# Rotary sines and cosines computed in the mixer's first phase, from a small load of their own

## The chip, the cores and the metric

One Trainium2 chip; the kernel uses one of its cores. The metric is device time in microseconds (us), the median of several runs. The engines are named as in the profile: PE is TensorE (PEld its weight loads), DVE is VectorE, ACT is ScalarE, POOL is GpSimd, and SP is SyncE, whose queue issues nearly all loads.

## The reference

A decoder block on 256 tokens of width 1024. All that the change touches is the rotary embedding of the retention branch:

```python
def rotary(x, positions):
    half = x.shape[-1] // 2
    inv = ROPE_BASE ** (-jnp.arange(half, dtype=jnp.float32) / half)
    ang = positions.astype(jnp.float32)[..., None] * inv
    cos = jnp.cos(ang)[:, :, None, :]
    sin = jnp.sin(ang)[:, :, None, :]
...
def mixer(...):
    proj = xm @ w_in        # 16 blocks of 512 columns, and 8 gate columns
    ml_qk = jax.nn.silu(causal_dwconv(ml_qk, conv_w, conv_b))
    h_ml = mlstm_chunkwise(...)          # needs the gates and the convolved q, k
    ret_q = rotary(ret_q ...); ret_k = rotary(ret_k ...)
    h_ret = retention_chunkwise(...)
...
x = x + gate_m * mixer(rmsnorm(x) * (1 + scale_m) + shift_m)
x = x + gate_f * moe(...)                # top 4 of 32 experts
```

The table of angles is 256 positions by 64 frequencies; in the kernel it is two tiles of 128 tokens side by side, 128x128.

## The kernel before

**Products.** Every weight tile of the mixer is split in two: ACT copies it to a rounded high half (`split_high`, L369, `partsa`), DVE subtracts to get the low half (`split_low`, L374, `partsb`), and PE multiplies high by high, low by high and high by low. Each half has a ring of four 128x512 slots, so ACT may run at most four splits ahead of PE. PE takes its products in the order in which they are written.

**First phase.** The modulation of the input comes in four steps `s`, each a quarter of the channels (two groups `k` of 128). A step multiplies the two groups that are ready by their rows of `qk0`, `qk1` (both L415 to L417) and `v0`, and in between makes the next two groups ready (`ada_mm`, `modulated`). Inside this phase PE, DVE and ACT run in the order in which the code is written (`tc.manual_schedule(engines=engines)`); an engine takes its instructions strictly in that order.

**Second phase.** Four more projections follow, `v1`, `rqk0`, `rqk1`, `rv0`, eight splits each (`projections`). Beside them runs `side`, a chain of generators: `gates` (the log-sigmoid of the forget gate: Exp, Ln, a reciprocal and two scans on DVE and ACT), `conv(1)`, `tables`, `gates_to_columns`, `weights_of_scores`, `scores`; PE takes one step of it after each projection product. In this phase only PE's order is written out; a scheduler sets the order on DVE and ACT, and SP's as well, and it may draw in work that is written later, such as `expert_biases` (three rounded levels `b` of the expert biases `braw`, L853, their differences L855, and 16 small copies issued on ACT, L857).

**The table.** `tables` casts the positions (`post`, an own load at L450) to `posf` (L525), multiplies them by the frequencies `inv`, reduces the angle to one turn, and takes two sines; sines and cosines land in the tile U1b. `inv` is 64 columns of the constants `cb`, which are loaded after the first phase, into memory that the first phase uses for other things. The angles live in a ring of three slots in U6b (`t2`). `rotated` reads the finished table.

**Loads.** SP issues loads one after another, each under one of eight completion semaphores in turn: the ninth load waits until the first has landed.

**After the mixer** come the router and 16 pairs of experts, whose weights (2 MB loads `gu`, `dn`) go into the mixer's weight slots as these come free.

Of the kernel before, what the change touches and what calls it, by code (L numbers as in the profile page):

```python
# [112 lines left out]
def block(ctx, tc, I, out, dbg=None):  # L113
    nc = tc.nc
    pe, dve, act, pool, sp = nc.tensor, nc.vector, nc.scalar, nc.gpsimd, nc.sync
# [111 lines left out]
    with ExitStack() as mctx:  # L227
# [43 lines left out]
        cb = U2b[:, 768:1988]  # L271
# [82 lines left out]
        qi = U1b[:, 512:1024].rearrange("p (h j) -> p h j", h=H)  # L354
        SR = U1b[:, 1024:1280]
        gc = U1b[:, 1280:1536].rearrange("p (c q) -> p c q", c=2)
        cs_ = U1b[:, 1536:1664].rearrange("p (t i) -> p t i", t=2)
        sn_ = U1b[:, 1664:1920].rearrange("p (t s i) -> p t s i", t=2, s=2)
        U3a = region("U3a", [128, 2048], "U3a")
        U3b = region("U3b", [128, 2048], "U3b")  # L360
        U4a = region("U4a", [128, 2056], "U4a")
# [90 lines left out]
        decay = cb[:, 128:640]  # L452
        kdec = cb[:, 640:644]
        qdec = cb[:, 644:1156]
        inv = cb[:, 1156:1220]

        wifs = sb(m, [128, 2, 416], "wifs", F32R, tag="gm")
        pool.memset(f32v(wifs), 0.0)
# [10 lines left out]
        def chain_of(*gens):  # L469
            for g in gens:  # L470
                yield from g
# [7 lines left out]
        def slow(gen):  # L479
            for _ in gen:  # L480
                yield
                yield
# [206 lines left out]
        with tc.manual_schedule(engines=engines):  # L689
# [53 lines left out]
            for s in range(4):  # L743
                ks = (2 * s, 2 * s + 1)
                p1 = [split(wq1[:, k:k + 1], f"qk1q{k}") for k in ks]
                for k, part in zip(ks, p0):
                    productsT(oqk[0], k, part)
                if s < 3:
                    scol = ada_mm(*SCALE[s + 1])
                else:  # L750
                    act.activation(warm, csil[:, 0:1], AF.Silu)
                    gate_weights()
                    side = conv(0)
                p2 = [split(wv0[:, k:k + 1], f"v0q{k}") for k in (ks[:1] if s < 3 else ks)]
                for k, part in zip(ks, p1):
                    productsT(oqk[1], k, part)
                if s == 3:
                    advance(side, 9)
                else:
                    p2.append(split(wv0[:, ks[1]:ks[1] + 1], f"v0q{ks[1]}"))  # L760
                    scol()
                    scale(s + 1)
                    shift = ada_mm(*SHIFT[s + 1])
                products1(ov0, ks[0], p2[0], hh)
                if s < 3:
                    p0 = [split(wq0[:, k:k + 1], f"qk0q{k}") for k in (2 * s + 2, 2 * s + 3)]
                    shift()
                    for k in (2 * s + 2, 2 * s + 3):
                        modulated(k)
                products1(ov0, ks[1], p2[1], hh)  # L770
        with tc.manual_schedule(engines={pe.engine}):
            held["wv1"] = wslot(win(3), "v1")
            sp.dma_start(cb, I["const_b"])
            for z in range(2):
                held[f"wrqk{z}"] = wslot(win(6 + z), f"rqk{z}")
            held["wrv0"] = wslot(win(8), "rv0")
            gate_products()
            main = projections()
            values(0, ov0)
            side = chain_of(gates(), slow(conv(1)), tables(), gates_to_columns(), weights_of_scores(), scores())  # L780
            for i in main:
                if i == 15:
                    side = both(side, rotated(0))
                if i == 23:
                    side = both(side, rotated(1))
                if i > 0:
                    advance(side)
            advance(side, 99)
            dbg("qT", qT)
            dbg("kT", kT)  # L790
            dbg("SR", SR)
            dbg("EX", EX4)
            dbg("Cs", Cs)
            dbg("nS", nS)
# [701 lines left out]
```

## Time and profile before

| | |
|---|---|
| median of 3 runs | 1243.28 us (1243.12 to 1244.7) |
| profiled execution | 1242.2 us, span 1240.4 us |
| busy, share of the span | PE 94%, DVE 39%, ACT 24%, POOL 1% |
| mean granted TensorE clock | 0.996 of full |
| bytes moved | 479.12 MB, 386 GB/s |

The span is what the profiler saw from the first to the last instruction; the profiled execution's own time is 1.8 us longer than it. The mixer takes the first 300 us, the experts the rest. A mean over the whole span says little about the change, which lies between 40 and 95 us; the stages there have to be read one by one.

### The profile page before, as it was taken

The numbers are of one execution on the slowest core, as the hardware profiler recorded it, in microseconds if no ns is written. First come the engines' busy times: TensorE is split into PE (matmuls) and PEld (weight loads), VectorE is DVE, ScalarE is ACT, GpSimd is POOL, SyncE is SP. The second block draws the span as 40 slices with busy tenths as digits, with TensorE's granted clock in tenths as the row PEclk, the third lists the DMA queues.
The fourth block names the chain that finished last, engine by engine and source line by source line (L and its number), as shares of the span: only waits on it lengthen the run. The fifth ranks groups of instructions, "written<-read, shape, count | busy, mean of one in ns | idle before, by whom it ended". The sixth has DMA issues, their size and how long they took to land.

```text
span 1240.4 us, 14605 instructions
## 1 busy us (share of the span) xinstructions
PE 1168.6 (94%) x5886; PEld 583.2 (47%) x5887; DVE 487.1 (39%) x1149; ACT 292.5 (24%) x575; POOL 7.8 (1%) x18
## 2 busy tenths in 40 slices
PE   8999999999999999999998989898989898989996
PEld 7878888888634334343332324232423233332333
DVE  5599889968422222222222222122212121312123
ACT  4585655565211101111110101010101010110112
POOL 0000000000000000000000000000000000000001
PEclk9999999999999999999999999999999999999999
DMA  9956789948999999999999999999999999999995
GB/s 365 368 181 210 273 301 350 365 174 334 350 430 428 428 427 428 427 428 429 425 427 429 427 428 426 427 430 427 426 428 429 427 426 429 427 427 428 426 421 214
DMA packets 44030, 479.12 MB, mean 386 GB/s; under 512 B 5554, under 2 KB 6514, under 8 KB 12980
## 3 DMA queue, kind: packets, MB, share of 16 engines
q1 hardware_dynamic: 42948, 477.01, 92.9%
q10 hardware_dynamic: 1008, 1.12, 0.3%
q8 instruction: 48, 0.79, 0.3%
q14 instruction: 26, 0.21, 0.1%
HBM read 476.46 MB, written 1.05 MB: 385 GB/s over the span
## 4 chain that ended last, share of the span: by engine, by line
DMA 54%; PE 43%; DVE 1%; ACT 1%; SPq 0%; issue 0%; ACTq 0%
PE gup L1260 10%; PE dnp L1297 5%; DMA gu123b<-in_w 3%; DMA gu83b<-in_w 3%; DMA gu63b<-in_w 3%; DMA gu103b<-in_w 3%; DMA gu151b<-in_w 3%; DMA gu91b<-in_w 3%; DMA gu131b<-in_w 3%; DMA gu143b<-in_w 3%; DMA dn131b<-in_w 3%; DMA dn71b<-in_w 3%; DMA gu111b<-in_w 3%; DMA dn51b<-in_w 3%; DMA dn91b<-in_w 3%; DMA gu71b<-in_w 3%
## 5 line engine op out<-in xcount | busy, mean ns | idle before, releaser
L1169 DVE TENSOR_SCALAR g<-gup 128x256 f32<-128x256 f32 x64 | 27.2, 425 | 344.0 <-PE gup L1260 344.0
L1249 ACT ACTIVATE aT<-aTp 128x256 f32<-128x256 f32 x64 | 24.5, 383 | 285.5 <-PE aTp L1248 285.5
L1170 ACT ACTIVATE sg<-g 128x256 f32<-128x256 f32 x64 | 26.7, 416 | 255.4 <-DVE g L1169 255.4
L1133 PEld LDWEIGHTS xgp<-oh,x 128*128 128x128 f32 x512 | 61.9, 191 | 49.6 <-issue 25.2
L1139 DVE TENSOR_SCALAR xg<-xgp,fsc,fsh 128x128 f32<-128x128 f32 x64 | 26.2, 409 | 146.7 <-ACT xg L1141 146.7
L1133 PE MATMUL xgp<-oh,x 128*128 128x128 f32 x512 | 73.7, 287 | 0.0
L1304 DVE SCALAR_TENSOR_TENSOR yp<-dnp,wsl,gf 128x512 f32<-128x512 f32 (+2 forms) x34 | 24.5, 719 | 111.9 <-PE dnp L1297 110.1
L1141 ACT ACTIVATE xg<-xgp,fsh,fsc 128x128 f32<-128x128 f32 x64 | 29.0, 453 | 150.6 <-PE xgp L1133 150.6
L1316 ACT ACTIVATE yph<-yp 128x512 fp32r<-128x512 f32 x31 | 19.5, 630 | 93.9 <-DVE yp L1304 93.9
L1248 PEld LDWEIGHTS aTp<-ca,a 128*128 128x128 f32 x128 | 13.7, 142 | 39.2 <-issue 39.2
L1173 DVE TENSOR_TENSOR a<-a,sg 128x256 f32<-128x256 f32 x64 | 27.2, 425 | 7.5 <-ACT sg L1170 1.0
L1172 DVE SCALAR_TENSOR_TENSOR a<-a,g 128x256 f32<-128x256 f32 x64 | 27.2, 425 | 2.1
L1322 PE MATMUL ya<-yph,ohT 128*128 128x512 f32 x62 | 27.8, 448 | 0.0
L1248 PE MATMUL aTp<-ca,a 128*128 128x128 f32 x128 | 27.4, 296 | 0.0
L1171 DVE TENSOR_SCALAR a<-gup 128x256 f32<-128x256 f32 x64 | 26.5, 415 | 0.0
L1159 DVE TENSOR_SCALAR ohT<-cwp 128x256 fp32r<-128x256 f32 x16 | 6.8, 424 | 49.1 <-PE cwp L1158 49.1
L1317 DVE TENSOR_TENSOR ypl<-yp,yph 128x512 fp32r<-128x512 f32 x31 | 21.3, 689 | 11.9 <-ACT yph L1316 11.9
L224 PE MATMUL gup<-bex,id 96*64 96x512 bf16 x128 | 25.1, 387 | 0.0
L1322 PE MATMUL ya<-ypl,ohT 128*128 128x512 f32 x62 | 24.6, 396 | 0.0
L1322 PEld LDWEIGHTS ya<-yph,ohT 128*128 128x128 f32 x62 | 11.6, 187 | 26.1 <-issue 24.3
L224 PEld LDWEIGHTS <-id 96*64 96x64 bf16 x196 | 11.6, 109 | 25.1 <-issue 22.3
L1125 DVE TENSOR_SCALAR oh<-ca,posm,rc 128x64 f32<-128x64 f32 x64 | 17.0, 309 | 4.6 <-PE xgp L1133 4.6
(902 smaller groups left out, 2317.6 us busy)
## 6 DMA issues: line engine op xcount, KB each, us to landing
gu00a<-in_w SPq DMA_DIRECT2D x1, 2048.0 KB, 7.7
gu00b<-in_w SPq DMA_DIRECT2D x1, 2048.0 KB, 7.5
gu01a<-in_w SPq DMA_DIRECT2D x1, 2048.0 KB
gu01b<-in_w SPq DMA_DIRECT2D x1, 2048.0 KB, 7.6
gu02a<-in_w SPq DMA_DIRECT2D x1, 2048.0 KB
gu02b<-in_w SPq DMA_DIRECT2D x1, 2048.0 KB, 12.6
gu03a<-in_w SPq DMA_DIRECT2D x1, 2048.0 KB
gu03b<-in_w SPq DMA_DIRECT2D x1, 2048.0 KB
```

Source lines behind the costliest of these rows:

```text
L224: pe.matmul(p[rows, :c1 - c0], id3[:, e:e + 1].to_broadcast([96, CAP]), bex[:, n, c0:c1], start=True, stop=False, skip_group_check=True)
L1133: pe.matmul(p[:, q * 128:(q + 1) * 128], x[:, t, k * 128:(k + 1) * 128], oh[:, t].rearrange("p q s -> p (q s)"), start=t == 0, stop=t == 1)
L1141: act.activation(xg[:, k], pq, AF.Identity, bias=fsh[:, k:k + 1], scale=fsc[:, k:k + 1])
L1169: dve.tensor_scalar(g[:r], v[:, 0], LIMIT, None, op0=OP.min)
L1170: act.activation(sg[:r], g[:r], AF.Sigmoid, scale=ALPHA)
L1171: dve.tensor_scalar(a[:r], v[:, 1], LIMIT, -LIMIT, op0=OP.min, op1=OP.max)
L1172: dve.scalar_tensor_tensor(a[:r], a[:r], 1.0, g[:r], op0=OP.add, op1=OP.mult)
L1173: dve.tensor_mul(a[:r], a[:r], sg[:r])
L1248: pe.transpose(p[:, q * 128:(q + 1) * 128], a[:, q * 128:(q + 1) * 128], ident)
L1260: pe.matmul(p[q * CAP:(q + 1) * CAP], xg[:, k, q * CAP:(q + 1) * CAP], w[q, k, slice(0, 512)], start=False, stop=k == 7, skip_group_check= ...
L1297: pe.matmul(p[q * CAP:(q + 1) * CAP, :c1 - c0], aT[:, k, q * CAP:(q + 1) * CAP], w[q, k, slice(c0, c1)], start=False, stop=k == 7, skip_gr ...
L1322: pe.matmul(yacc[t][n], ohT[:, t * 128:(t + 1) * 128], part, start=pair == i == 0, stop=i == 1 and pair >= NP - 2, skip_group_check=True)
```

## The change

The table gets a tile of its own, `rot`, instead of a part of U1b, and the frequencies get a tile and a load of their own, issued right behind the load of the positions. All of `tables()` is run at the end of step `s == 1` of the first phase, behind `modulated` of that step and ahead of the splits of `qk1` of the next one. The chain `side` has one generator less.

```diff
--- before.py
+++ after.py
@@ -354,8 +354,9 @@
         qi = U1b[:, 512:1024].rearrange("p (h j) -> p h j", h=H)
         SR = U1b[:, 1024:1280]
         gc = U1b[:, 1280:1536].rearrange("p (c q) -> p c q", c=2)
-        cs_ = U1b[:, 1536:1664].rearrange("p (t i) -> p t i", t=2)
-        sn_ = U1b[:, 1664:1920].rearrange("p (t s i) -> p t s i", t=2, s=2)
+        rot = sb(m, [128, 384], "rot")
+        cs_ = rot[:, 0:128].rearrange("p (t i) -> p t i", t=2)
+        sn_ = rot[:, 128:384].rearrange("p (t s i) -> p t s i", t=2, s=2)
         U3a = region("U3a", [128, 2048], "U3a")
         U3b = region("U3b", [128, 2048], "U3b")
         U4a = region("U4a", [128, 2056], "U4a")
@@ -452,7 +453,8 @@
         decay = cb[:, 128:640]
         kdec = cb[:, 640:644]
         qdec = cb[:, 644:1156]
-        inv = cb[:, 1156:1220]
+        inv = sb(m, [128, 64], "inv")
+        sp.dma_start(inv, I["const_b"][:, 1156:1220])
 
         wifs = sb(m, [128, 2, 416], "wifs", F32R, tag="gm")
         pool.memset(f32v(wifs), 0.0)
@@ -768,6 +770,9 @@
                     for k in (2 * s + 2, 2 * s + 3):
                         modulated(k)
                 products1(ov0, ks[1], p2[1], hh)
+                if s == 1:
+                    for _ in tables():
+                        pass
         with tc.manual_schedule(engines={pe.engine}):
             held["wv1"] = wslot(win(3), "v1")
             sp.dma_start(cb, I["const_b"])
@@ -777,7 +782,7 @@
             gate_products()
             main = projections()
             values(0, ov0)
-            side = chain_of(gates(), slow(conv(1)), tables(), gates_to_columns(), weights_of_scores(), scores())
+            side = chain_of(gates(), slow(conv(1)), gates_to_columns(), weights_of_scores(), scores())
             for i in main:
                 if i == 15:
                     side = both(side, rotated(0))
```

On DVE in the first phase the code's order decides. These are its rows before, at the end of step s=1: `hb` is the low half of the modulated input, `partsb<-wfirst1b` the low halves for `qk1` of step s=2.

```order
L440 TENSOR_TENSOR hb<-U2b,ha 128x256
L374 TENSOR_TENSOR partsb<-wfirst1b,partsa 128x512 x2
L313 COPY U6b<-ada_544 128x128
L374 TENSOR_TENSOR partsb<-wfirst2b,partsa 128x512 x2
L303 TENSOR_TENSOR mod<-adac_583,cols 128x2
```

And with the change, at the same place (`post` are the positions, `rot` the table):

```order
L441 TENSOR_TENSOR hb<-U2b,ha 128x256
L527 CAST posf<-post 128x2
L530 TENSOR_SCALAR U6b<-inv,posf 128x64 x2
L535 TENSOR_SCALAR U6b<-U6b 128x128
L536 TENSOR_SCALAR U6b<-U6b 128x128
L538 SCALAR_TENSOR_TENSOR U6b<-U6b 128x128 x3
L540 TENSOR_SCALAR U6b<-U6b 128x128
L545 TENSOR_TENSOR U6b<-U6b 128x128
L546 TENSOR_SCALAR rot<-U6b 128x128
L547 TENSOR_SCALAR rot<-rot 128x2x64
L375 TENSOR_TENSOR partsb<-wfirst1b,partsa 128x512 x2
```

The twelve instructions of the table now stand between `hb` and the two low halves; the row `CAST` needs the positions' load, and the row behind it that of `inv`.

On DVE in the second phase the scheduler decides. Before, from the reciprocal of the gates on (`nS` and `U1a` hold gates, `partsb` are low halves for `v1` and `rqk0`, `U2b` the convolution):

```order
L562 RECIPROCAL nS<-nS 4x256
L374 TENSOR_TENSOR partsb<-v1b,partsa 128x512
L563 TENSOR_TENSOR nS<-nS 4x256
L374 TENSOR_TENSOR partsb<-rqk0a,partsa 128x512
L565 TENSOR_TENSOR nS<-nS 4x256
L374 TENSOR_TENSOR partsb<-rqk0a,partsa 128x512
L566 SCALAR_TENSOR_TENSOR nS<-nS 4x256
L504 SCALAR_TENSOR_TENSOR U2b<-qk1p_294,cols,U2b 128x254
L572 SCALAR_TENSOR_TENSOR U1a<-nS 4x128 x2
L504 SCALAR_TENSOR_TENSOR U2b<-qk1p_294,cols,U2b 128x255
L573 SCALAR_TENSOR_TENSOR U1a<-fi,bif,U1a 4x256
L374 TENSOR_TENSOR partsb<-rqk0a,partsa 128x512
```

With the change:

```order
L564 RECIPROCAL nS<-nS 4x256
L375 TENSOR_TENSOR partsb<-v1b,partsa 128x512
L565 TENSOR_TENSOR nS<-nS 4x256
L375 TENSOR_TENSOR partsb<-v1b,partsa 128x512
L567 TENSOR_TENSOR nS<-nS 4x256
L506 SCALAR_TENSOR_TENSOR U2b<-qk1p_297,cols,U2b 128x253
L568 SCALAR_TENSOR_TENSOR nS<-nS 4x256
L506 SCALAR_TENSOR_TENSOR U2b<-qk1p_297,cols,U2b 128x254
L574 SCALAR_TENSOR_TENSOR U1a<-nS 4x128 x2
L506 SCALAR_TENSOR_TENSOR U2b<-qk1p_297,cols,U2b 128x255
L575 SCALAR_TENSOR_TENSOR U1a<-fi,bif,U1a 4x256
L375 TENSOR_TENSOR partsb<-rqk0a,partsa 128x512
```

One more low half of `v1` now stands behind the reciprocal, and the first of `rqk0` has moved from the second place behind it to the last row shown, behind most of the gates' chain. Further on, ahead of the first low half of `rqk0b`, stand three differences of `braw` that before stood behind all of `rqk1`.

On ACT in the second phase, before, from the first high half of `v1b` to the logarithm (L557 is the gates' Exp, L560 their Ln, L499 the Silu of the convolution):

```order
L369 ACTIVATE partsa<-v1b 128x512
L499 ACTIVATE U3a<-U2b 128x256
L497 ACTIVATE U2b<-qk1p_295,cols 128x256
L369 ACTIVATE partsa<-v1b 128x512
L557 ACT_TABLE_LOAD
L557 ACTIVATE nS<-nS 4x256
L369 ACTIVATE partsa<-v1b 128x512 x2
L560 ACT_TABLE_LOAD
L560 ACTIVATE nS<-nS 4x256
L499 ACT_TABLE_LOAD
L499 ACTIVATE U3a<-U2b 128x256
```

With the change (line numbers up by two; L858 and L862 are `expert_biases`):

```order
L858 ACTIVATE b_2322<-braw_1247 128x512
L499 ACTIVATE U2b<-qk1p_297,cols 128x256
L862 DMA bex<-b_2322 32x512 x3
L501 ACTIVATE U3a<-U2b 128x256
L862 DMA bex<-b_2322 32x512
L370 ACTIVATE partsa<-v1b 128x512
L559 ACT_TABLE_LOAD
L559 ACTIVATE nS<-nS 4x256
L501 ACT_TABLE_LOAD
L501 ACTIVATE U3a<-U2b 128x256
L370 ACTIVATE partsa<-v1b 128x512
L562 ACT_TABLE_LOAD
```

A bias level and four copies have come in ahead of the first high half of `v1b`, and one Silu now stands between Exp and Ln, with a table load of its own.

## Rows read from the trace of the kernel before

**Rows 1.** The page: its span, and the shares of the chain that ended last

```profile
span 1240.4 us, 14605 instructions
...
DMA 54%; PE 43%; DVE 1%; ACT 1%; SPq 0%; issue 0%; ACTq 0%
```

**Rows 2.** Stages of the mixer: length, busy time per engine (instructions), PEclk, DMA share

```profile
70.00:85.00 15.00, 12.29 (x52) 9.03 (x51) 13.79 (x30) 12.65 (x22) 0.00 (x0) 1.00 0.43 139
85.00:300.00 215.00, 214.27 (x1017) 177.39 (x1016) 192.47 (x386) 124.97 (x215) 0.00 (x0) 1.00 0.75 279
```

**Rows 3.** TensorE in order of time, first products of `qk1` in step s=2

```profile
45.21 0.28 PE L416 MATMUL qk1p<-ha,partsb 128*128 128x256 f32 x1
45.33 0.28 PE L417 MATMUL qk1p<-hb,partsa 128*128 128x256 f32 x1
```

**Rows 4.** VectorE in order of time: first low half for those products; the cast

```profile
41.88 0.69 DVE L374 TENSOR_TENSOR partsb<-wfirst1b,partsa 128x512 fp32r<-128x512 f32 x1
...
57.74 0.16 DVE L525 CAST posf<-post 128x2 f32<-128x2 int32 x1
```

**Rows 5.** SyncE's queue in order of time, around the positions' load

```profile
40.86 0.40 SPq L450 DMA_DIRECT2D post<-in_positions  x1
42.20 0.36 SPq L170 DMA_DIRECT2D v1a<-in_win  x1
```

**Rows 6.** DMA issues from 30 to 46 us: KB, us from issue to landing

```profile
v1a<-in_win SPq DMA_DIRECT2D x1, 1024.0 KB, 5.3
...
post<-in_positions SPq DMA_DIRECT2D x1, 1.0 KB, 4.3
```

**Rows 7.** VectorE on the tile U6b, 66 to 94 us: ns min/median/max

```profile
L536 DVE SCALAR_TENSOR_TENSOR U6b<-U6b x3: 269/273/273, 89.8 to 91.1; 128x128 f32<-128x128 f32 x3
...
L528 DVE TENSOR_SCALAR U6b<-U2b,posf x2: 232/240/247, 69.3 to 87.8; 128x64 f32<-128x64 f32 x2
...
L533 DVE TENSOR_SCALAR U6b<-U6b x1: 208/208/208, 88.6 to 88.6; 128x128 f32<-128x128 f32 x1
```

**Rows 8.** ScalarE on the tile U6b, 66 to 94 us

```profile
L540 ACT ACTIVATE U1b<-U6b x1: 293/293/293, 92.7 to 92.7; 128x128 f32<-128x128 f32 x1
```

**Rows 9.** ScalarE in order of time, its first two entries

```profile
0.78 1.28 ACT L690 ACT_TABLE_LOAD   x1 [0.64 <-PEq L1484]
3.08 0.21 ACT L690 ACTIVATE csil<-ca 128x8 f32<-128x8 f32 x1 [1.02 <-DMA ca<-in_const_a]
```

**Rows 10.** TensorE in order of time, two of its waits in the second phase

```profile
80.80 0.50 PE L387 MATMUL rqk_p<-partsb,ha 128*128 128x512 f32 x1 [1.18 <-DVE partsb L374]
...
84.58 0.50 PE L387 MATMUL rqk_p<-partsb,ha 128*128 128x512 f32 x1 [0.63 <-DVE partsb L374]
```

**Rows 11.** ACT and DVE in order of time, from the gates' Exp to their reciprocal

```profile
69.81 1.15 ACT L369 ACTIVATE partsa<-v1b 128x512 fp32r<-128x512 f32 x2
...
70.98 1.28 ACT L560 ACT_TABLE_LOAD   x1
...
72.28 0.42 ACT L560 ACTIVATE nS<-nS 4x256 f32<-4x256 f32 x1
...
70.29 0.48 DVE L504 SCALAR_TENSOR_TENSOR U2b<-qk1p,cols,U2b 128x253 f32<-128x253 f32 x1
...
72.72 1.74 DVE L562 RECIPROCAL nS<-nS 4x256 f32<-4x256 f32 x1 [0.78 <-ACT nS L560]
```

**Rows 12.** The tile b (bias levels), 55 to 130 us: ns min/median/max

```profile
L857 ACTq DMA_DIRECT2D bex<-b x16: 514/515/605, 90.3 to 129.0; - x16
L853 ACT ACTIVATE b<-braw x5: 615/622/632, 89.6 to 127.6; 128x512 bf16<-128x512 f32 x3, 64x512 bf16<-64x512 f32 x2
L855 DVE TENSOR_TENSOR braw<-braw,b x3: 630/680/687, 104.4 to 126.0; 128x512 f32<-128x512 f32 x2, 64x512 f32<-64x512 f32 x1
```

**Rows 13.** The end of the run, columns as in rows 2

```profile
1230.00:1232.00 2.00, 0.40 (x4) 0.21 (x2) 1.02 (x6) 0.55 (x3) 0.00 (x0) 1.00 0.03 8
...
1236.00:1238.00 2.00, 0.00 (x0) 0.00 (x0) 0.00 (x0) 0.00 (x0) 0.00 (x0) 0.50 0.78 309
```

## The prediction

> **What bounds the kernel now.** I read the page first. The chain of work that ended last is DMA for 54% and PE for 43% [rows 1]: the expert stage streams its weights to the end, and before it PE sets the pace. The expert loads start when mixer slots come free, so a microsecond won or lost in the mixer moves the whole stream, one for one. The table by stage shows where the mixer can move. From 85 to 300 us PE is busy 214.27 of 215.00; from 70 to 85 us it idles 2.71 of 15.00, while DVE is busy 13.79 [rows 2]. PE's own rows say what for: low halves that DVE had not finished, 1.18 us at 80.80 and 0.63 us at 84.58 [rows 10]. The table's costly part stands at 88 to 94 us in the run before [rows 7], where PE has no idle time that could be given back.
>
> **Term 1: the table in the first phase.** Added are one load, and on DVE twelve instructions; on ACT two sines and a table load. They stand ahead of the low halves for `qk1` of step s=2. The first of these starts at 41.88 now [rows 4], and PE uses it at 45.21 [rows 3]: 2.6 us of slack beyond its 0.69.
>
> DVE's first new row casts the positions. Their load is issued at 40.86 [rows 5] and takes 4.3 us [rows 6], behind large loads in the same queue, so it lands at 45.2. Nothing ahead of it on SP changes, so DVE, which goes on in order, stands still from about 42.0 to 45.2 although it has nothing else to wait for. The frequencies follow on SP at the place that the load of `v1a` holds now, 42.20 [rows 5], when the next of the eight semaphores is free. No row shows this load. Lower bound: it lands with the positions, 45.2. Upper bound: 5.3 us like `v1a`, 1 MB issued at the same moment [rows 6], that is 47.5. It is 32 KB, so I take it near the lower end, 45.4. The loads behind it move back by one place; that is hidden, since `v1a` has landed at 47.5 and its first low half comes after the cast at 57.74 [rows 4, 6].
>
> From 45.4 the DVE chain is dependent, so durations add, each from its twin of the run before [rows 7]: two products with the frequencies, the second overlapped (0.25 + 0.15), two of 0.21, three of 0.27, a clamp of 0.21: 1.84, and some 0.2 for eight handovers. 47.45. Then ACT: the sine whose result is squared starts about 0.2 behind the first and takes 0.29 [rows 8]: 48.0. The table load costs nothing if it runs ahead of its operand. The very first one did: it ran at 0.78, and the instruction behind it then sat idle for 1.02 until its load [rows 9]. The lower bound is 0, the upper 1.28 [rows 11]; I take 0, as ACT is idle there while it waits for DVE. DVE then squares (about 0.27) and makes cosines and the negated sines (0.21 each, overlapped), to 48.7 [rows 7]; ACT has the high half by 48.5, DVE the low half at 48.7 + 0.7 = 49.4. PE's second matmul of `qk1` starts at 49.4 instead of 45.21: **4.2 us late**. The bounds are 4.0 and 6.3 from the two landings, 7.6 if the table load waits too.
>
> PE cannot make this up. The splits, convolutions and gates behind it depend on what PE does in this phase, and the four slots keep ACT and DVE from running far ahead.
>
> **Term 2: the second phase.** Taken from it are the cast (0.16), the twelve-row chain of some 2.6, and two sines. All but the cast and one product (0.25) stood at 88 us or later, where PE is full: worth nothing. Ahead of the first low half of `rqk0b`, for which PE waits at 84.58, the new order puts three bias differences, 0.63 to 0.69 each [rows 12], 2.0 in all, that stood at 104 us and later. Less the 0.41 removed that is +1.6 us on DVE, in its busiest stretch.
>
> Second, the gates. The reciprocal overwrites what Ln reads, so it waits for ACT: 0.78 us now [rows 11]. Between the end of Exp and the end of Ln ACT did two splits, one table load and Ln, 1.15 + 1.28 + 0.42 = 2.85. With the change it does a table load, a Silu, a split, another table load and Ln: 1.28 + 0.42 + 0.57 + 1.28 + 0.42 = 3.97 [rows 11], so 1.1 more. DVE filled that time before with two taps of the convolution, 0.48 each [rows 11], that now come ahead of Exp. Its idle time grows by 1.1 + 0.96, about 2.0. Together **3.6 us** by which the low half of `rqk0b`, and PE with it, comes later. From there PE is full and the lead that DVE regains is not used.
>
> ScalarE: Activation LUTs of the Trainium skill (section What ACT_TABLE_LOAD costs) would make each switch of tables dearer, about 2.66 us, of which 1.38 is a drain behind the load. The rows show no drain: the load at 70.98 takes 1.28 and its activation starts at 72.28 [rows 11]. By the page the one extra load would add 1.4 us to the sum; I go by the row.
>
> The bounds of term 2 are -2.7 (all of PE's idle time from 70 to 85 us is recovered [rows 2], because the relief came earlier than the order shows) and +5 (the four copies and the bias levels on ACT, 0.51 and 0.62 each [rows 12], delay high halves too). The two sums above go row by row through the new order, so I take 3.6.
>
> **Sum.** 4.2 + 3.6 = 7.8 on the profiled execution's 1242.2 (span 1240.4 and 1.8 around it) is 1250.0. The median of the runs shown, 1243.28, is 1.1 higher, so I name 1251.0.
>
> **Rivals.**
> *Only the first term.* The second phase hides its new waits under others: 1243.3 + 4.2 = 1247.5. For it: DVE and ACT both have small gaps from 70 to 85 us [rows 2]. Against: the gaps of DVE are waits for ACT, and both get more work.
>
> *The clock falls in the stall.* TensorE stands nearly still for some 4 us. The rows show one fall: PE had its last work in 1230 to 1232 at clock 1.00, and the clock is 0.50 in 1236 to 1238 [rows 13], which is 1.2 of 2.4 GHz. If the stall does the same, the 24 `qk1` products behind it, 0.12 apart [rows 3], take 2.9 us more: 1254. Against: PE was idle longer there. TensorE: Matmul & The Clock Gate of the Trainium skill (section The HAM clock gate) says that an idle array falls to half rate and gets the full rate back after sustained work; the end of the run agrees, and no row shows whether this stall is enough.
>
> *Not slower: the relief reaches PE.* Place: the low halves from 70 to 85 us. If DVE without the table delivers them in time, PE's 2.71 us of idle time go, and with the stall of 4.2 the time is 1244.8, within 0.2%. It decides from a gain of 1.7 us on. To end faster, the positions and frequencies would also have to have landed by 42: then the table costs 0.9 beyond the slack of term 1 (0.2 + 2.0 on DVE, 0.6 for the sines, 0.7 for the last three, against 2.6), and the time is 1241.5, still inside the bound. Against: the removed rows stood behind that stretch.
>
> **Chances.** Forecast, both terms (including a late `inv` or the dearer table load, up to 1254): 0.55. Only the first: 0.22. Clock: 0.13. Relief: 0.10, of which 0.02 stands for a gain of over 0.2%, which needs 0.7 us more than the best case just named. The range 1247.0 to 1254.5 leaves out the relief and what of the clock and a late landing adds up. What a measurement of this kernel can tell from no change is about 0.2%, 2.5 us. So slower 0.90, same 0.08, faster 0.02.
>
> **What would show it.** Right: DVE idle before the cast until about 45.2, released by the load of the positions or of `inv`; the table load on ACT near 41.2, with no wait; PE's `qk1` low product of s=2 at about 49.4; the first `rqk0b` low product near 92.4 instead of 84.58; PE full from there on, and the last 900 us the same but shifted. Wrong: the cast at 42; a granted clock below 1.00 from 49 us on; the first `rqk0b` product within 4.5 us of 84.58, which would cancel term 2; or new waits for loads in the mixer, whose order on SP has changed.

## The result and the profile after

The median after is 1254.2 us (six runs, 1253.33 to 1255.34), against 1243.47 us before (six runs beside them, 1243.12 to 1244.7). The ratio is 1.0084, with a 95% interval of 1.0074 to 1.0094: slower by 10.7 us. The profiled execution of after took 1254.67 us, so its span is 12.3 us longer than that of before [rows 1]; two single executions differ by their own scatter too. One execution of e7 below took 5756 us, at full clock and for no known cause, and its median and ratio go by the other five. The page after, its span and the shares of the chain that ended last:

```profile
span 1252.7 us, 14602 instructions
...
DMA 57%; PE 39%; DVE 2%; ACT 2%; issue 0%; SPq 0%; ACTq 0%; DVEq 0%
```

The loss lies in the mixer. Stages of after, columns as in [rows 2]:

```profile
45.00:50.00 5.00, 1.00 (x10) 0.36 (x2) 3.52 (x14) 1.55 (x4) 0.00 (x0) 0.73 0.92 320
50.00:55.00 5.00, 5.00 (x27) 5.00 (x27) 1.97 (x4) 1.31 (x3) 0.00 (x0) 0.59 0.99 397
55.00:60.00 5.00, 5.00 (x36) 3.51 (x37) 3.02 (x9) 2.59 (x6) 0.31 (x1) 1.00 0.79 264
70.00:85.00 15.00, 11.97 (x55) 8.99 (x54) 10.21 (x18) 11.87 (x20) 0.96 (x1) 1.00 0.55 204
```

Two things are new. PE does 1.00 us of work in 45 to 50, and its granted clock is 0.73 there and 0.59 in the next five. From 70 to 85 DVE is busy for 10.21 us instead of 13.79 [rows 2]: it has less to do and waits, so another engine is late.

**The first phase.** VectorE of after in order of time, from the cast to the first low half of `qk1` for s=2:

```profile
45.58 0.17 DVE L527 CAST posf<-post 128x2 f32<-128x2 int32 x1 [3.32 <-DMA post<-in_positions]
...
48.59 0.29 DVE L545 TENSOR_TENSOR U6b<-U6b 128x128 f32<-128x128 f32 x1 [0.57 <-ACT U6b L543]
...
49.19 1.28 DVE L375 TENSOR_TENSOR partsb<-wfirst1b,partsa 128x512 fp32r<-128x512 f32 x2
```

DVE stood still for 3.32 us. What it waited for, in SyncE's queue and in the view of DMA issues (KB, us to landing):

```profile
41.40 0.40 SPq L451 DMA_DIRECT2D post<-in_positions  x1
42.67 0.36 SPq L457 DMA_DIRECT2D inv<-in_const_b  x1
```

```profile
inv<-in_const_b SPq DMA_DIRECT2D x1, 32.0 KB, 3.1
...
post<-in_positions SPq DMA_DIRECT2D x1, 1.0 KB, 4.2
```

41.40 + 4.2 = 45.6 and 42.67 + 3.1 = 45.8: the two loads land nearly together, and the chain of the table runs from there to 49.2. ScalarE's table load for the sines cost nothing, as it ran ahead of its operand:

```profile
41.46 1.28 ACT L542 ACT_TABLE_LOAD   x1
48.05 0.31 ACT L542 ACTIVATE rot<-U6b 128x128 f32<-128x128 f32 x1 [5.30 <-DVE U6b L540]
```

TensorE behind it, the products of `qk1` for s=2 that answer to [rows 3], the last of them, and what follows:

```profile
49.12 0.58 PE L416 MATMUL qk1p<-ha,partsa 128*128 128x256 f32 x1 [3.77 <-ACT partsa L370]
49.93 0.58 PE L417 MATMUL qk1p<-ha,partsb 128*128 128x256 f32 x1 [0.22 <-DVE partsb L375]
50.30 0.41 PE L418 MATMUL qk1p<-hb,partsa 128*128 128x256 f32 x1
50.52 0.41 PE L416 MATMUL qk1p<-ha,partsa 128*128 128x256 f32 x1
...
54.13 0.28 PE L418 MATMUL qk1p<-hb,partsa 128*128 128x256 f32 x1
54.25 0.28 PE L416 MATMUL qk1p<-ha,partsa 128*128 128x256 f32 x1
...
54.61 0.50 PE L301 MATMUL adac<-ca,U6b 128*128 128x1 f32 x4
```

The second product starts at 49.93 instead of 45.21. The starts then lie 0.21 apart until 53.9, and 0.12 apart after that: the clock's lower level, 1.2 of 2.4 GHz. Of the 24 products, 18 went by at that pace. From 49.93 to the `adac` behind these products it is 4.68 us; before, it was 2.75 (45.21 to 47.96), so the clock cost 1.9.

**The second phase.** ScalarE of after, from the first bias level to the gates' Ln (the counterpart of [rows 11]):

```profile
70.49 0.63 ACT L858 ACTIVATE b<-braw 128x512 bf16<-128x512 f32 x1 [0.41 <-DMA braw<-in_bgu]
...
71.15 2.77 ACTq L862 DMA_DIRECT2D bex<-b  x3
73.97 0.42 ACT L501 ACTIVATE U3a<-U2b 128x256 f32<-128x256 f32 x1 [2.39 <-DVE U2b L506]
...
75.25 1.28 ACT L559 ACT_TABLE_LOAD   x1
76.55 0.42 ACT L559 ACTIVATE nS<-nS 4x256 f32<-4x256 f32 x1
...
79.23 1.28 ACT L562 ACT_TABLE_LOAD   x1
80.53 0.42 ACT L562 ACTIVATE nS<-nS 4x256 f32<-4x256 f32 x1
```

The first level waits 0.41 us for its own load. Three DMA issues then fill ScalarE's queue until 73.92 (71.15 + 2.77), and the Silu behind them starts at 73.97. Its idle time of 2.39 us is put down to a tap of DVE (a step of the convolution), since the profile counts no issue as work. That tap had ended by about 72.3, so some 1.7 us of the wait are the issues'; the row above it shows what the engine did. All issues, in the groups of the tile `b` [rows 12], as ns min/median/max:

```profile
L862 ACTq DMA_DIRECT2D bex<-b x18: 514/515/1496, 71.2 to 117.6; - x18
```

One takes 515 ns as a rule, and the third of these 1496. There were 18 in the kernel before too (two of them behind the window of [rows 12]), so only their place is new. With them ScalarE was full from 70 to 85: 11.87 us of busy time, 2.77 of issues, and 0.57 for a fourth at 73.98 make 15.2 of 15.00, the little too much being overlap. Before, all issues stood behind 90 us [rows 12].

TensorE's waits of this phase, the last two of which answer to [rows 10]:

```profile
79.27 0.49 PE L387 MATMUL v_p<-partsa,ha 128*128 128x512 f32 x1 [1.23 <-ACT partsa L370]
...
83.49 0.50 PE L388 MATMUL v_p<-partsb,ha 128*128 128x512 f32 x1 [1.34 <-DVE partsb L375]
...
88.84 0.50 PE L388 MATMUL rqk_p<-partsb,ha 128*128 128x512 f32 x1 [2.33 <-DVE partsb L375]
...
92.62 0.50 PE L388 MATMUL rqk_p<-partsb,ha 128*128 128x512 f32 x1 [0.63 <-DVE partsb L375]
96.41 0.50 PE L388 MATMUL rqk_p<-partsb,ha 128*128 128x512 f32 x1 [0.23 <-DVE partsb L375]
```

The last two are smaller than their twins before. The loss shows in the three ahead of them, at 79 to 89 us. The first low product of `rqk0b` starts at 96.41 instead of 84.58, 11.8 us later.

To compare runs I read three places of each trace, on TensorE in order of time: the first product of the gates (the end of the first phase), the last product of `rqk0` and `rqk1`, and the last product of the second `rv` block; the differences are the lengths of the stretches. Each trace is of one execution. Behind the last `rv` product the traces of all runs take 1103.0 to 1106.9 us to the end of the span, so that medians and places can differ by some microseconds. e3 and e7 stand in the text.

| run | median us | ratio, interval | gates | to last rqk | to last rv | last rv |
|---|---|---|---|---|---|---|
| before | 1243.47 | | 61.57 | 47.65 | 26.43 | 135.65 |
| after | 1254.2 | 1.0084 [1.0074, 1.0094] | 68.21 | 53.71 | 25.61 | 147.53 |
| e1 | 1245.04 | 1.0008 [0.9999, 1.0017] | 63.18 | 48.38 | 27.83 | 139.39 |
| e2 | 1249.09 | 1.0036 [1.0023, 1.0049] | 68.20 | 48.34 | 26.61 | 143.15 |
| e4 | 1254.34 | 1.0073 [1.0058, 1.0088] | 68.90 | 52.61 | 27.49 | 149.00 |
| e5 | 1243.83 | 1.0004 [0.9995, 1.0013] | 62.04 | 48.36 | 27.83 | 138.23 |
| e6 | 1242.67 | 0.9992 [0.9984, 1.0001] | 62.50 | 48.39 | 26.61 | 137.50 |
| e8 | 1249.56 | 1.0053 [1.0040, 1.0066] | 67.33 | 49.62 | 25.65 | 142.60 |
| e9 | 1246.91 | 1.0028 [1.0017, 1.0039] | 66.23 | 48.35 | 26.61 | 141.19 |
| e10 | 1253.23 | 1.0073 [1.0059, 1.0087] | 66.23 | 53.83 | 25.66 | 145.72 |
| e11 | 1243.74 | 1.0002 [0.9993, 1.0011] | 62.49 | 47.49 | 27.49 | 137.47 |

After against before: +6.64 in the first phase, +6.06 to the last `rqk` product, -0.82 behind it. That is 11.9, of the 12.3 by which the spans differ. Kernels that share the code of the first phase end it up to 1.6 us apart (after, e2, e4 and e8), so a smaller difference in one trace proves little.

### The profile page after: what moved, and what is told of

It is laid out like the page before. It is cut to its first block, busy times and chain, and to the rows that moved or that the text cites. A ratio compares the mean times of both kernels' runs of the same rounds, so it can differ in the third digit from the quotient of the medians.

```text
span 1252.7 us, 14602 instructions
## 1 busy us (share of the span) xinstructions
PE 1170.0 (93%) x5886; PEld 583.1 (47%) x5887; DVE 487.9 (39%) x1149; ACT 295.8 (24%) x577; POOL 7.8 (1%) x18
## 4 chain that ended last, share of the span: by engine, by line
DMA 57%; PE 39%; DVE 2%; ACT 2%; issue 0%; SPq 0%; ACTq 0%; DVEq 0%
PE gup L1265 10%; PE dnp L1302 5%; DMA gu83b<-in_w 3%; DMA gu123b<-in_w 3%; DMA gu151b<-in_w 3%; DMA gu63b<-in_w 3%; DMA gu103b<-in_w 3%; DMA dn91b<-in_w 3%; DMA dn51b<-in_w 3%; DMA dn131b<-in_w 3%; DMA dn111b<-in_w 3%; DMA gu143b<-in_w 3%; DMA gu71b<-in_w 3%; DMA gu131b<-in_w 3%; DMA dn71b<-in_w 3%; DMA gu111b<-in_w 3%
## 5 line engine op out<-in xcount | busy, mean ns | idle before, releaser
L1322 DVE TENSOR_TENSOR ypl<-yp,yph 128x512 fp32r<-128x512 f32 x31 | 21.3, 688 | 11.9 <-ACT yph L1321 11.9
```

## The experiments

Each ratio is to runs of the kernel before on the same chip (their medians 1243.24 to 1243.75). e1 to e4 shared one chip, e5 to e8 another, e9 to e11 a third.

### e1: the small loads early

```diff
         sp.dma_start(rv, I["rows"])
+        post = sb(m, [128, 2], "post", I32)
+        sp.dma_start(post, I["positions"][0].rearrange("(t p) -> p t", p=128))
+        inv = sb(m, [128, 64], "inv")
+        sp.dma_start(inv, I["const_b"][:, 1156:1220])
...
-        sp.dma_start(post, I["positions"][0].rearrange("(t p) -> p t", p=128))
...
-        sp.dma_start(inv, I["const_b"][:, 1156:1220])
```

> Edit: the loads of the positions and of the inverse frequencies are issued right after the load of the rows instead of behind the big streams; all else as in the changed kernel. It also lets the scheduler put the three bias differences and most bias copies behind the second phase's first weights again, as in the kernel before. Theory A (the loss has three parts: 4.4 us of waiting for the two late loads, 2 us of TensorE products at the lower clock that follow from that wait, 5 us of a second phase in which ScalarE's early bias copies push the gates back): all three go, 1242.5 to 1245.5 us, granted clock 1.00 through the first phase, no wait of VectorE before the table's cast. Rival B (the second phase loses its 5 us because the side chain is one step shorter, whatever the loads do): only 6.4 us come back, 1247 to 1249 us, and the first low product of rqk0b still starts 4 to 5 us later relative to the end of the first phase than in the kernel before. Rival C (the 12 table operations on VectorE and the two sines on ScalarE delay the first phase by themselves): 1246 to 1247 us, with TensorE waiting 2 to 3 us behind them in the first phase.

1245.04 us; the interval of the ratio holds 1. Two late loads of 33 KB together are thus the root of nearly the whole loss: with them early the wait, the fall of the clock and the scheduler's early bias work are all gone. What is left in the first phase is the table's own time. VectorE, and then TensorE, in e1:

```profile
42.42 0.16 DVE L527 CAST posf<-post 128x2 f32<-128x2 int32 x1
...
45.98 1.28 DVE L379 TENSOR_TENSOR partsb<-wfirst1b,partsa 128x512 fp32r<-128x512 f32 x2
```

```profile
45.91 0.39 PE L420 MATMUL qk1p<-ha,partsa 128*128 128x256 f32 x1 [0.31 <-ACT partsa L374]
46.72 0.39 PE L421 MATMUL qk1p<-ha,partsb 128*128 128x256 f32 x1 [0.42 <-DVE partsb L379]
```

The chain takes 3.56 us from the cast to the low half; the slack takes most of it, and TensorE waits 0.31 + 0.42. That is rival C's mechanism at a third of its price.

### e2: the bias loads held back

```diff
-        braw = [sb(m2, [rows, 512], f"braw{rows}") for rows in (128, 64)]
-        sp.dma_start(braw[0], I["bgu"])
-        for n in range(2):
-            sp.dma_start(braw[1][n * 32:(n + 1) * 32], I["b_down"][0, :, n * 512:(n + 1) * 512])
...
         some(99)
+        braw = [sb(m2, [rows, 512], f"braw{rows}") for rows in (128, 64)]
+        sp.dma_start(braw[0], I["bgu"])
+        for n in range(2):
+            sp.dma_start(braw[1][n * 32:(n + 1) * 32], I["b_down"][0, :, n * 512:(n + 1) * 512])
         expert_biases()
```

> Edit: the changed kernel with the three loads of the expert biases written just ahead of the expert-bias work instead of ahead of the second retention half; the late small loads, the wait and the table's place stay. ScalarE's order in the second phase then has its first bias copy behind the Ln load, where the changed kernel has it ahead of the Exp load. Theory A: the first phase stays as late as in the changed kernel (about 6.6 us at its end, with the lower clock), and of the second phase's 5 us 3 to 5 come back: 1249 to 1251 us. Rival B (the shorter side chain, or the late start itself, is what costs the second phase): nothing comes back, 1253 to 1255 us.

1249.09: 5.1 us of 10.7 come back, with the first phase as late as in after (68.20). The stretch from the gates to the last `rqk` product falls from 53.71 to 48.34, that is to within 0.7 us of the kernel before, and the stretch behind it grows by 1.0. Rival B falls: neither the shorter chain nor the late start costs the second phase anything near 5 us; the bias work does, with the order that the scheduler builds around it on ACT and DVE, which e2 changes too.

### e3 and e7: fillers that did more than fill

```diff
+                if s == 2:
+                    for _ in range(8):
+                        pe.matmul(busy[:, :128], ones, ones, start=True, stop=True)
                 for k, part in zip(ks, p1):
                     productsT(oqk[1], k, part)
```

> Edit: 8 products of ones by ones (nothing reads them) on TensorE ahead of the second half's qk1 products, in the place where TensorE waits in the changed kernel; VectorE's, ScalarE's and the load queue's orders are the same as in the changed kernel, row for row. Theory A: the wait stays, but the granted clock stays at 1.00, the 24 qk1 products go by at 0.12 us instead of 0.21, and the first phase ends about 2 us earlier than in the changed kernel: 1251.7 to 1252.8 us. Rival D (the slow products cost nothing in the end, since the second phase waits on ScalarE's chain anyway): the clock stays up and the time stays at 1253.5 to 1255. If the filler runs past the wait it costs instead: above 1255.

1254.28 (1.0075, 1.0060 to 1.0090). The clock stayed at 1.00 from 45 to 55, the products went by at 0.12, and the gates started at 66.26, 1.95 us earlier than in after. The last `rqk` product came only 0.5 earlier (121.45 against 121.92). ScalarE shows what took the gain:

```profile
70.74 0.63 ACT L861 ACTIVATE b<-braw 128x512 bf16<-128x512 f32 x1 [2.60 <-DMA braw<-in_bgu]
```

The first bias level stood still for its load until 70.74, as late as in after (70.49), though the load was issued at 61.25 instead of 63.20. The kernel had changed at another place as well. TensorE in e3, in the first half:

```profile
18.05 0.66 PE L715 MATMUL hT<-ca,y 128*128 128x128 f32 x4 [1.53 <-ACT U1a L722]
```

Before and after have no such wait. `busy` is the tile of the warm-up products, and a second use keeps one of the two PSUM buffers of its pool taken through the whole first half. The `ada` products ahead of the wait start 1.95 us later for it (46.23 against 44.28), which the wait for the small loads hides. e7 puts the same filler into e2:

> Edit: e2 (bias loads held back) and the 8 filler products of e3 together. In e3 the filler kept the clock up and the first phase ended 2 us earlier, but the second phase gave it back, because ScalarE's first bias copy waited for its load until 70.74 us whatever TensorE did. Theory A: with that copy away the 2 us reach the end: 1246.5 to 1247.5 us, against 1249.1 in e2. Rival D (the products at the lower clock never cost the end anything): 1248.5 to 1249.7 us, as e2.

1249.4 (1.0040, 1.0027 to 1.0053). Its first half was hit harder: the clock fell already from 15 to 25 us (0.73 and 0.59), and the `ada` products ahead of the wait started at 48.95 instead of 44.03. That took all that the filler won, and the gates start at 68.31, as in e2. So e3 tells the clock's price for the end of the first phase alone, and e7 does not tell it; e9 tells what of it reaches the end of the mixer.

### e4: an empty step in the side chain

```diff
-            side = chain_of(gates(), slow(conv(1)), gates_to_columns(), weights_of_scores(), scores())
+            side = chain_of(gates(), slow(conv(1)), iter([0]), gates_to_columns(), weights_of_scores(), scores())
```

> Edit: the changed kernel with an empty step in the side chain at the place from which the table was taken, so that the projections' products meet the gates, the scores and the rest at the same steps as in the kernel before; the bias copies stay ahead as in the changed kernel. Theory A: no gain, 1253.5 to 1255.5 us. Rival B (the chain that is one step shorter costs the second phase): 3 to 5 us come back, 1249 to 1251 us.

1254.34, as after. It shortens the stretch to the last `rqk` product by 1.1 us and lengthens the next by 1.9. The missing step is no cause.

### e5 and e6: the table in a gap, and the biases held too

```diff
                 for k, part in zip(ks, p0):
                     productsT(oqk[0], k, part)
+                if s == 1:
+                    rest = tables()
+                    next(rest)
...
                     shift = ada_mm(*SHIFT[s + 1])
+                    if s == 1:
+                        for _ in rest:
+                            pass
...
-                if s == 1:
-                    for _ in tables():
-                        pass
```

e5 is this with e1's early loads.

> Edit: early loads as in e1, and the table's first part (nine VectorE operations, two sines) moved from the end of the first half to a place behind the qk0 products of s=1, where VectorE sat idle for 1.95 us ahead of its copy of ada in the kernel before, its last three operations behind the shift row of s=1. Theory A: the 1.1 us by which e1's qk1 products of s=2 waited for the table's own operations are gone, the first phase ends 0.3 to 0.6 us later than in the kernel before, and the time is that of the kernel before within 0.2% (1242.5 to 1244.5), since the second phase did not gain from being rid of the table in e1 either. Rival E (VectorE's relief of 3 us in the second phase does reach TensorE once nothing hides it): 1240 to 1242 us. Rival C (the table's operations cost the first phase wherever they stand): 1244.5 to 1246 us.

1243.83: the time of before. TensorE in e5 has no wait at the place in question:

```profile
45.48 0.39 PE L420 MATMUL qk1p<-ha,partsa 128*128 128x256 f32 x1
45.70 0.28 PE L421 MATMUL qk1p<-ha,partsb 128*128 128x256 f32 x1
```

The table is computed, in its own tile and from its own load, for nothing that the medians can tell. And the second phase, rid of twelve VectorE instructions, is not shorter: 48.36 and 27.83 against 47.65 and 26.43 before. Rival E falls. e6 adds the edit of e2:

> Edit: e5, and the three loads of the expert biases written just ahead of the expert-bias work as in e2, so that no bias copy stands ahead of the Cs copies on ScalarE and no bias difference among VectorE's low parts of rqk0 and rqk1. If VectorE's and ScalarE's load is what paces the second phase (theory A taken further): 1239 to 1242 us. If TensorE's products set it, or the bias work comes back later: 1242.5 to 1244.5, as e5.

1242.67, and the interval of the ratio, 0.9984 to 1.0001, holds 1. Against e5 it is 1.2 us, and the traces have them between the last `rqk` and the last `rv` product (27.83 to 26.61), to where the scheduler had moved the bias work. It is the fastest kernel of the study, but not one that this measurement tells from the kernel before.

### e8: the bias writes on another queue

```diff
-                        act.dma_start(bex[i * 32:(i + 1) * 32, 4 * j + n], b3[n * 32:(n + 1) * 32, i])
+                        pool.dma_start(bex[i * 32:(i + 1) * 32, 4 * j + n], b3[n * 32:(n + 1) * 32, i])
```

> Edit: the changed kernel with the writes of the split biases issued from GpSimd's queue instead of ScalarE's. ScalarE's first bias copy still waits for its load ahead of the Exp load, and two more bias copies stand behind it, but no DMA issue does (three of them held ScalarE's queue for 2.77 us in the changed kernel). If the issues are the price: 1250.5 to 1252.5 us. If the copy's wait for its load and the copies themselves are the price: 1253.5 to 1255.5 us.

1249.56: 4.6 us come back, more than was expected of the issues. ScalarE in e8, from the first bias level (its wait for its load is still there) to the Exp load:

```profile
69.40 0.63 ACT L858 ACTIVATE b<-braw 128x512 bf16<-128x512 f32 x1 [0.18 <-DMA braw<-in_bgu]
...
72.97 1.28 ACT L559 ACT_TABLE_LOAD   x1
```

From the level to the load it is 3.57 us, with two more levels of 0.5 between, against 4.76 in after (70.49 to 75.25). The stretch to the last `rqk` product is 4.1 us shorter than in after, of the 5.4 that e2 wins by moving everything. The levels and their differences are still there. So the price is mostly that of the issues in ScalarE's queue, together with the order that the scheduler builds around them: in e8 it also moved the first low halves of `rqk0a` from 88.11 us to 83.53, right behind the gates' reciprocal, as in e1 and e2. No run keeps the one and changes the other. The first phase of this run also ended 0.9 us earlier (67.33), though the edit does not touch it: the small loads were issued 0.57 earlier in this trace, and fewer products were slow. That is within the scatter named above, so I count the 4.1 us of the second phase and not the 4.6. DMA: Bandwidth & Descriptors of the Trainium skill (section Issuing engines are not separate DMA queues) says that issuing from several engines saves only the sequencer's time to initiate a DMA, usually small against the DMA itself. Here that time, 0.5 to 1.5 us apiece for the first four of 18 issues, is what decides, on an engine with little time to spare.

### e9 and e10: fillers in a tile of their own

```diff
+                if s == 2:
+                    spare = tr("spare")
+                    for _ in range(14):
+                        pe.matmul(spare[:, :128], ones, ones, start=True, stop=True)
```

> Edit: e2 (bias loads held back) and 14 filler products in TensorE's wait, this time into a PSUM tile taken only there. In e3 and e7 the fillers wrote the tile of the warm-up products at the kernel's start, which kept one of the two buffers of the pool that ada, adac and the transposes share through the whole first half; TensorE waited there for the other (1.53 us at a transpose, 0.25 at each ada), and the first half came 2 to 5 us later, so those two runs don't tell the clock's price. Theory A: the clock stays at 1.00, the qk1 products of s=2 go by at 0.12 us, the gates' products start near 66.2 us instead of 68.2, and the 2 us reach the end: 1246.5 to 1247.7 us. Rival D (the products at the lower clock cost the end nothing): 1248.7 to 1249.7 us.

TensorE in e9 (the trace has two records for each of the 14 fillers), and its stages:

```profile
45.32 3.39 PE L760 MATMUL spare<-ones 128*128 128x128 f32 x28
48.97 0.38 PE L416 MATMUL qk1p<-ha,partsa 128*128 128x256 f32 x1 [0.26 <-ACT partsa L370]
49.78 0.38 PE L417 MATMUL qk1p<-ha,partsb 128*128 128x256 f32 x1 [0.42 <-DVE partsb L375]
50.00 0.28 PE L418 MATMUL qk1p<-hb,partsa 128*128 128x256 f32 x1
50.12 0.28 PE L416 MATMUL qk1p<-ha,partsa 128*128 128x256 f32 x1
```

```profile
45.00:50.00 5.00, 4.32 (x39) 3.61 (x32) 3.68 (x14) 1.55 (x4) 0.00 (x0) 1.00 0.88 297
50.00:55.00 5.00, 5.00 (x47) 4.27 (x47) 2.43 (x7) 1.78 (x5) 0.31 (x1) 1.00 1.00 423
```

The wait is where it was in e2 (49.84 there, 49.78 here), the clock stays up, and the gates start 1.97 us earlier. The gain arrives whole at the last `rv` product: 143.15 to 141.19. The medians differ by 2.2 (1249.09 to 1246.91), or by 1.8 when each is taken against the kernel before on its own chip; the intervals of the two ratios overlap, so the trace carries this number.

> Edit: the changed kernel and the same 14 fillers into a tile of their own; VectorE, ScalarE and the load queue keep the changed kernel's order row for row. Theory A as it stands after e3: the first phase ends 2 us earlier, but ScalarE's first bias copy still waits for its load near 70.5 us ahead of the Exp load, so that at most 0.5 us of the two reach the end: 1253.3 to 1254.3 us. Rival D2 (the bias load comes earlier too, and the 2 us come through): 1251.7 to 1252.7 us.

1253.23, just below theory A's range and above D2's; the interval is too wide to choose. The trace chooses: the last `rv` product comes 1.81 us earlier than in after. ScalarE's bias level did not wait until 70.5:

```profile
69.54 0.63 ACT L862 ACTIVATE b<-braw 128x512 bf16<-128x512 f32 x1 [1.43 <-DMA braw<-in_bgu]
```

Its load was issued at 61.22 instead of 63.20. The level so comes 0.95 us earlier than in after, and the three issues behind it took 1.88 us together instead of 2.77, which is the rest (the Exp load stands at 73.42 instead of 75.25). So e10 prices the clock only together with these two. In e3 the same load was issued as early and its level came no earlier, so the reading of e3, that the landing took the gain, stands for that run; when this load lands is not settled by its issue alone.

### e11: all of it, with the loads behind those of x

e6, the empty step of e4, and the two loads behind those of x instead of ahead:

```diff
         for t in range(2):
             sp.dma_start(x[:, t], I["x"][0, t * 128:(t + 1) * 128])
+        post = sb(m, [128, 2], "post", I32)
+        sp.dma_start(post, I["positions"][0].rearrange("(t p) -> p t", p=128))
+        inv = sb(m, [128, 64], "inv")
+        sp.dma_start(inv, I["const_b"][:, 1156:1220])
```

> Edit: e6 with the two small loads behind those of x instead of ahead of them (in e1, e5 and e6 the square sums of x came later, and the first ada products waited 1.19 us for them where the changed kernel waited 0.83), and the empty step in the side chain of e4. If the start costs what the rows say, the first phase ends 0.4 us earlier than in e6, and with the products meeting the gates at the steps of the kernel before the second phase is no longer than there: 1241.0 to 1242.4 us, faster than both kernels. If the second phase is set by TensorE's own products and the bias work only moves: 1242.4 to 1243.8.

1243.74, not told from before. The later place of the loads won nothing at the end of the first phase that one trace can show (62.49 against 62.50), and what the empty step wins up to the last `rqk` product it gives back up to the last `rv` product.

## Why the prediction was nearly right, point by point

**Side and size.** Slower was right. The time, 1254.2, is 3.2 us over the 1251.0 named and just inside the range's upper end. That it lies inside is partly luck: the upper end was set for a late `inv` or a dearer table load, and neither happened. The clock and a longer wait of VectorE filled that room instead.

**Term 1, 4.2 us late.** Right in place, cause and size. The second product of `qk1` lies 5.65 us behind the start of the `ada` products ahead of it (44.28) and lay 1.22 behind them before, so the delay is 4.43. Both loads landed in the expected order (45.6 and 45.8, named 45.2 and 45.4), the table load ran ahead, and from the cast to the low half the chain took 3.6 us, where the sum had 3.3 (45.4 to 48.7). The runs agree: e9, with held biases and the clock up, against e6, where the biases are held, the loads early and the table in the gap, is 1246.91 - 1242.67 = 4.2 us, or 4.1 with each against the kernel before on its own chip.

**The clock.** This was the step taken too low: a chance of 0.13 for a thing that happened. The prediction's own sign of being wrong, a granted clock below 1.00 from 49 us on, came true. The rival priced it at 2.9 us for 24 products; it is 1.9 to 2.0 (after, and e9 against e2), since only the 18 products until 53.9 went by slowly. The argument against it was that the rows show one fall, at the end of the run, where TensorE had been idle longer [rows 13]. But the trace of the kernel before has another, in the midst of the experts' work, behind a wait of 2.37 us:

```profile
1029.36 1.38 PE L1260 MATMUL gup<-gu123b,xg 128*64 128x512 f32 x4 [2.37 <-DMA gu123b<-in_w]
```

```profile
1030.00:1031.00 1.00, 1.00 (x5) 0.29 (x2) 0.00 (x0) 0.00 (x0) 0.00 (x0) 0.50 1.04 442
```

That wait is shorter than the stall that was forecast, and it speaks for the rival. In after the clock fell in a wait of 3.77 us. The length of one wait does not settle it: the wait for the first low half of `rqk0a` is 2.33 us in after and e10 and 2.34 in e4, and the clock behind it stays at 1.00 in after, while the stages of e10 and e4 show 0.77 and 0.67. TensorE: Matmul & The Clock Gate of the Trainium skill (section The HAM clock gate) says that an idle array drops to half rate and has the full rate back after sustained work; this trace agrees, with 0.21 against 0.12 us.

**Term 2, 3.6 us.** Right in its first part and mis-sized in its second. The term measures 5.2 in the traces (6.06 to the last `rqk` product, 0.82 given back) and 5.1 on the medians as they stand (after against e2). From the first product of the gates to the first low half of `rqk0b`, in before, after and e8, columns as in [rows 2]:

```profile
61.57:83.86 22.29, 20.21 (x98) 16.14 (x96) 20.65 (x46) 19.25 (x34) 0.96 (x1) 1.00 0.43 146
```

```profile
68.21:95.67 27.46, 21.45 (x97) 15.71 (x95) 22.20 (x47) 23.02 (x39) 0.96 (x1) 1.00 0.53 177
```

```profile
67.33:90.75 23.42, 20.29 (x98) 16.21 (x96) 22.60 (x47) 21.84 (x38) 8.93 (x17) 1.00 0.69 226
```

VectorE's own work grows by 1.55 us, and the sum had 1.6 for it. Its idle time grows from 1.64 to 5.26, by 3.6, where the sum had 2.0. The step that failed is this one: VectorE's wait for ACT was counted only from Exp to Ln, and what had come in on ACT ahead of Exp, a level and four copies, which are DMA issues, stood only in the upper bound of +5, at 0.51 and 0.62 each from medians [rows 12]. ScalarE had no room for them: in the stretch of before that answers to 70 to 85 us of after, 63.4 to 78.4, it was busy for 14.08 of 15.00 us. Level and issues took 4.0 of its time (0.63 + 2.77 + 0.57), so Exp came later and VectorE waited. In e8 VectorE has as much work as in after, and its idle time there is 0.8 us. So the wait goes with the issues, and with the order that comes with them.

**The table load.** By ScalarE: Activation LUTs of the Trainium skill (section What ACT_TABLE_LOAD costs) a switch has a drain of 1.38 us beside the load. The rows of after show none, neither ahead of the load nor behind it: the split ahead of the load at 75.25 ends at 75.24, the loads at 75.25 and 79.23 take 1.28, and their activations start at 76.55 and 80.53.

**The removed rows, worth nothing.** Right, as far as the medians tell: e5 has them out of the second phase with no wait for the table in the first, and its time is that of before (0.9995 to 1.0013). For the same reason the rival in which the relief reaches PE is out.

**Together.** 4.4 + 1.9 + 5.2 in the traces, and 0.3 by which the `ada` products ahead of the wait start later: 11.9 with rounding. On the medians, each against the kernel before on its own chip, it is 4.1 + 1.8 + 5.4 (e6 to e9, e9 to e2, e2 to after); by the ratios of the table, which are those of means, 4.5 + 1.0 + 6.0. The parts of the medians are thus sure to about a microsecond, and the traces agree with them within that. Before lies some 0.6 to 1.0 above e6, hence the 10.7. The forecast had 4.2 + 0 + 3.6.

**What stays open.** Why the scheduler brings the bias work forward was not taken apart. What is shown is that it does so with the late loads and not with the early ones (e1, e5), and that it costs what e2 wins. In after it issues the load of the biases at 63.20, ahead of that of `rv0a`, and the first level stands at 70.49; in e1 the load is issued at 79.20, behind both loads of `rv0`, and the level stands at 90.0. Why one issue on ScalarE took 1496 ns and others 515 is open as well; in e3 and e10 the same three took 1.88 us together. And e8 moves all 18 issues at once and changes the scheduler's order with them, so that neither the share of the first three nor that of the order is known.

## What to carry to other kernels

Before an operation is moved forward, look at where its operands' loads stand in the issuing queue: a 1 KB load behind megabyte loads lands 4 us after its issue, and an engine in order stands still for it with all that is behind it. A wait of TensorE costs more than its length when the clock falls in it; here it was 4.4 us of wait and 2 us of slow products. Look for such falls in the whole trace of the kernel before, not only in the stage at hand. Where a scheduler orders the rest, read its new order on every engine and add DMA issues on a compute engine to its busy time, which does not count them.

## What the hardware showed that I had not expected

- The granted clock fell in a wait of TensorE of 3.77 us, in the kernel before in one of 2.37, and behind waits of 2.33 to 2.34 us in some runs and not in others. Products that nobody reads, 3.39 us of them, kept it at 1.00 and bought 2 us (e9).
- A DMA issue on ScalarE took up to 1496 ns, against a median of 515, and the activations behind it waited.
- A tile used a second time held one of two PSUM buffers between its uses, and a filler meant to help slowed the first half by 2 (e3, where another wait hid it) to 5 us (e7).
